# Seven products instead of eight in five chunks of two projections of a two-layer encoder

## The chip, the cores and the metric

The kernel runs on one core of a Trainium2 chip. The metric is the device time of one execution, in microseconds. Before the change it was measured three times: 2317.64, 2317.91 and 2318.44 us, median 2317.91. The five engines are called by the short names of the profile: PE (matrix multiply), DVE (VectorE), ACT (ScalarE), POOL (GpSimd) and SP (the engine that issues most transfers).

## What is computed

A trunk of two layers over x of 2048 tokens by 1024 features, in float32. Layer 0 mixes with a short gated convolution and a Fourier mixer, layer 1 with grouped-query attention:

```python
x = x + short_conv_fourier_mixer(rms_norm(x, norm_even), w_in_even, conv_w, w_out_even)
x = x + gqa_axial_mixer(rms_norm(x, norm_odd), w_in_odd, q_gain, k_gain, w_out_odd)
return rms_norm(x, final_norm)
```

The change concerns three of the four big matrix products in it: the output projection of layer 0 (`y @ w_out_even`, 2048x1024 by 1024x1024), the input projection of layer 1 (`h @ w_in_odd`, to q, k, v and the gate z, 2560 columns) and the output projection of layer 1 (1024 columns). The input projection of layer 0 already uses the scheme that the change brings to others.

## The kernel before, in words

**Chunks.** All big projections are cut into chunks of 1024 tokens (two blocks of 512, numbered `pr`) by 512 output columns. The contraction has 1024 features. So a chunk multiplies a 2x2 block matrix of activations (A11, A12, A21, A22: token block, then half of the features) by a 2x2 block matrix of weights (W11 to W22: half of the features, then half of the columns). `multiply` (L332) makes one block product: 4 slices of the contraction, 2 tiles of PSUM, and 3 matmuls each, since a float32 operand is kept as a rounded high word and a remainder (`split`, L40, a cast on ACT and a subtraction on DVE) and `mm3` (L56) adds high x high, high x low and low x high. That is 24 matmuls.

**Two ways to do a chunk.** `plain` (L368) makes the 8 block products of the schoolbook rule. `product` (L387) makes 7, by Strassen's rule in Winograd's form: beside A11, A12 and A22 it takes four combined activations, s3 = A11 - A21, s1 = A21 + A22, s2 = s1 - A11 = A22 - s3 and s4 = A12 - s2, and beside W11, W21 and W22 four combined weights t1 to t4 (`weight_ops`, L288, makes them with subtractions on POOL). The results of its products are summed on DVE (`sums`, L392) into tiles of the pool "e", before they are handed to the chunk's `out`, without PSUM for three of the four blocks. Before the change `product` is used in layer 0's input projection alone; the output projections and layer 1's input use `plain`.

**Rooms.** The pool "big" (tag "S") has 9 rooms of 16 KB a partition. An operand (high and low word) takes one. Two rooms are the rings "r" and "o": "r" has 4 places of 128x1024 for raw weights, "o" gives passing tiles by `pair` (L184), strictly in turn; in layer 0's input it has 3 places, the fourth holding a temporary of the combined weights, and after `renew` (L161) it has 4. The weights in use lie in the pool "w", 8 tiles (4 operands) in layers 0 and 1, 6 and two of another pool in the last projection. PSUM has 8 banks.

**What is done between products.** After each product `follow` (L361) calls a hook of the chunk and one step of `queue`. `queue_weights` (L310) puts the steps of the next chunk's weights there: the loads, and each of the four splits just after the product that uses the old block of that place for the last time. `reload` (L263) gives the hooks that load and split the next two token blocks. In layer 1, g1 scales the weights in the split (L285, L286).

**What sets the order.** The order of PE is that of the program text. The other engines and SP are ordered by a planner that simulates the program with its own times and prefers earlier text; every engine then runs its instructions strictly in that order. `issue_after` and `high_priority` bend this at a few places.

**The chunks in order.** Layer 0's output (`layer0_out`, L969) runs (pr, column half) = (0,0), (0,1), (1,0), (1,1). `out_chunk` (L933) loads the residual into a place of "o", adds it to PSUM on DVE (L945), stores x1, squares on ACT (L962) and adds up on POOL (L964). Layer 1's input (`layer1_in`) runs, for each pr, z2, kv, q0, q1, z3 (numbers 2, 4, 0, 1, 3); the very last, z3 of pr 1, is split into a batch and fillers that end inside the first steps of attention. In q and kv chunks the activations are the stationary side; `rope` works on DVE, ACT and POOL, and transposes on PE (`turn`, L1058) follow three or four products later. Layer 1's output (`layer1_out`) starts right at the end of attention and ends with a chunk cut by columns.

Of the kernel before, what the change touches and what calls it, by code (L numbers as in the profile page):

```python
# [23 lines left out]
P = 128  # L24
# [123 lines left out]
class Pairs:  # L148
# [7 lines left out]
    def __init__(self, c):  # L156
        self.c, self.nc = c, c.tc.nc
        self.A, self.pending, self.queue, self.rooms = {}, [], [], []
        self.renew(3)

    def renew(self, o=4):  # L161
        self.A.clear()
        self.size = {"r": 4, "o": o}
# [99 lines left out]
    def reload(self, src, name):  # L263

        return {i: lambda b=b: self.load_block(src, b, name) for i, b in ((0, "11"), (2, "12"), (4, "21"), (5, "22"))}
# [22 lines left out]
    def weight_ops(self, src, name, raw_tiles=None, lo_engs={}):  # L288
# [19 lines left out]
        return W, {"11": s11, "t2": s_t2, "t3": s_t3, "t1": s_t1, "21": s21, "t4": s_t4, "22": s22}  # L308

    def queue_weights(self, src, name, g):  # L310

        W, raw = {}, {}

        def start():
            raw.update(self.raw_weights(src))

        def step(b):
            return lambda: self.split_weights(W, b, raw[b], name, g=g)
# [4 lines left out]
        self.queue.extend([start, wait, step("11"), step("21"), wait, wait, step("12"), step("22")])  # L323
        return W

    def all_weights(self, src, name, lo_engs={}):
        W, steps = self.weight_ops(src, name, lo_engs=lo_engs)
# [59 lines left out]
    def product(self, W, out, name, hooks={}):  # L387
# [482 lines left out]
def layer0_out_start(c):  # L870
# [62 lines left out]
def out_chunk(c, pr, mc, W, hooks, conv_first, src, dst, acc, nm):  # L933
# [5 lines left out]
    def out(block, t, ps):  # L939
# [26 lines left out]
    st.plain(W, out, f"po{nm}_{pr}_{mc}_", hooks, conv_first)  # L966


def layer0_out(c):  # L969
# [801 lines left out]
```

## Time and profile before

| what | value |
|---|---|
| median of three runs | 2317.91 us |
| the profiled execution | 2315.25 us, its span 2313.5 us |
| layer 0's output projection | 583 to 760 us of the span |
| layer 1's input projection, up to attention | 760 to 1203 us |
| attention | 1203 to 2120 us |
| layer 1's output projection | 2120 us to the end |
| granted clock of PE, mean | 0.991 |
| bytes moved by DMA | 413.98 MB |

The profile shows one execution. Busy time is the union of an engine's instructions in a stretch; a wait is the idle time of an engine ahead of an instruction, put down to what ended it. Stretches are given in us from the start of the span. For a transfer, the time from its issue to its landing is given.

### The profile page before, as it was taken

The page shows a single profiled execution, that of the slowest core. Times are in us where ns is not written, and L with a number is a line of the kernel's source. Part 1 is how long each engine was busy: PE and PEld are TensorE (multiplying, and loading weights), DVE is VectorE, ACT ScalarE, POOL GpSimd, SP SyncE. Part 2 cuts the span into 40 slices and gives each one's busy share as a digit, 9 for nine tenths or more (in the row PEclk, how much of TensorE's full clock was granted, in tenths as well). Part 3 has the DMA queues.
Part 4 walks back from the last instruction along what each step waited for, and adds up shares of the span by engine and source line. Part 5 has one row for each costly group of instructions (what it writes and reads, how often), then busy time and mean ns, then how long its engine had stood idle before and what let it go on. Part 6 is the DMA issues. An engine that isn't in the chain of part 4 may idle for free. (4 is left out here: it accounts for less than half of the span.)

```text
span 2313.5 us, 34304 instructions
## 1 busy us (share of the span) xinstructions
PE 2265.7 (98%) x12450; PEld 1920.2 (83%) x12450; DVE 1530.3 (66%) x2479; ACT 1198.4 (52%) x2638; POOL 574.8 (25%) x408
## 2 busy tenths in 40 slices
PE   9999999998999999999999999999999999999998
PEld 7877778886888899889987888888888888888887
DVE  7967667679542545424537887788788778878235
ACT  5442333224332335424537777777777777777212
POOL 3566535444222222203211110000000110003212
PEclk9999999998999999999999999999999999999999
DMA  4244742265856533533465555555555555558653
GB/s 166 81 151 169 249 137 74 64 248 186 277 182 191 151 133 122 164 110 127 145 221 216 204 203 192 200 202 195 195 200 201 193 198 200 204 183 295 210 190 129
DMA packets 247992, 413.98 MB, mean 179 GB/s; under 512 B 24848, under 2 KB 144784, under 8 KB 246032
## 3 DMA queue, kind: packets, MB, share of 16 engines
q1 hardware_dynamic: 240944, 404.11, 51.0%
q0 software_dynamic: 1008, 6.55, 0.8%
q8 instruction: 99, 1.62, 0.3%
q10 hardware_dynamic: 5872, 1.14, 0.2%
q14 instruction: 69, 0.57, 0.1%
HBM read 190.92 MB, written 86.59 MB: 120 GB/s over the span
## 5 line engine op out<-in xcount | busy, mean ns | idle before, releaser
L1320 DVE TENSOR_REDUCE mx<-s 128x1 f32<-128x512 f32 x512 | 350.9, 686 | 173.7 <-PE s L60 173.3
L1339 ACT ACTIVATE praw<-s,nb,qs 128x512 f32<-128x512 f32 x512 | 400.6, 798 | 19.5 <-DVE nb L1329 13.4
L1362 ACT CAST pr<-t 128x512 fp32r<-128x512 f32 x512 | 290.0, 599 | 182.3 <-PE t L1350 182.3
L1366 DVE TENSOR_TENSOR pr<-t,pr 128x512 fp32r<-128x512 f32 x512 | 329.1, 679 | 7.5 <-ACT pr L1362 7.3
L1350 PEld LDWEIGHTS t<-ident_r,P 128*128 128x128 f32 x2048 | 202.0, 140 | 36.8 <-DVE pr L1366 1.1
L58 PE MATMUL s<-kv,aq 128*128 128x512 f32 x512 | 211.5, 413 | 3.1 <-DMA aq<-qT 1.9
L58 PE MATMUL o<-pr,kv 128*128 128x512 f32 x512 | 212.1, 414 | 0.1
L1350 PE MATMUL t<-ident_r,P 128*128 128x128 f32 x2048 | 203.8, 243 | 0.9 <-DVE pr L1366 0.9
L60 PE MATMUL o<-pr,kv 128*128 128x512 f32 x512 | 202.5, 395 | 0.0
L60 PE MATMUL s<-kv,aq 128*128 128x512 f32 x512 | 202.5, 395 | 0.0
L59 PE MATMUL o<-pr,kv 128*128 128x512 f32 x512 | 202.1, 395 | 0.0
L59 PE MATMUL s<-kv,aq 128*128 128x512 f32 x512 | 201.3, 393 | 0.0
L1411 POOL TENSOR_TENSOR az<-az,lb 128x512 f32<-128x512 f32 x32 | 61.8, 1930 | 442.6 <-DMA lb<-ld 407.3
L964 POOL TENSOR_TENSOR acc<-acc,sq 128x512 f32<-128x512 f32 x48 | 69.2, 1442 | 214.5 <-ACT sq L962 196.3
L60 PEld LDWEIGHTS o<-pr,kv 128*128 128x128 f32 x512 | 96.2, 188 | 23.3
L60 PEld LDWEIGHTS s<-kv,aq 128*128 128x128 f32 x512 | 96.4, 188 | 22.6
L58 PEld LDWEIGHTS s<-kv,aq 128*128 128x128 f32 x512 | 95.9, 187 | 22.1 <-ACT praw L1339 3.2
L1418 POOL TENSOR_TENSOR az<-az,oc 128x512 f32<-128x512 f32 x32 | 42.2, 1318 | 286.2 <-ACT oc L1417 286.1
L1339 ACT ACTIVATION_READ_ACCUMULATOR praw<-s,nb,qs 128x1 f32 x512 | 112.2, 219 | 0.0
L59 PEld LDWEIGHTS s<-kv,aq 128*128 128x128 f32 x512 | 96.6, 189 | 17.3
L59 PEld LDWEIGHTS o<-pr,kv 128*128 128x128 f32 x512 | 96.5, 188 | 17.2
L58 PEld LDWEIGHTS o<-pr,kv 128*128 128x128 f32 x512 | 96.0, 187 | 16.9 <-ACT oc L1417 0.2
(643 smaller groups left out, 5821.9 us busy)
## 6 DMA issues: line engine op xcount, KB each, us to landing
P<-praw SPq DMA_DIRECT2D x256, 512.0 KB, 3.2
ring_r<-w SPq DMA_DIRECT2D x80, 512.0 KB, 3.6
ring_o<-x_T SPq DMA_DIRECT2D x32, 512.0 KB, 4.8
ring_r<-wo SPq DMA_DIRECT2D x32, 512.0 KB, 7.0
qT<-ring_o SPq DMA_DIRECT2D x64, 256.0 KB, 2.8
aq<-qT SPq DMA_DIRECT2D x31, 512.0 KB, 4.6
x1T<-po_t SPq DMA_DIRECT2D x16, 512.0 KB, 3.9
a_x<-x1T SPq DMA_DIRECT2D x16, 512.0 KB, 4.4
```

What stands on the lines that cost most here:

```text
L58: nc.tensor.matmul(ps, lh, rh, start=first, stop=False, skip_group_check=shared)
L59: nc.tensor.matmul(ps, lh, rl, start=False, stop=False, skip_group_check=shared)
L60: nc.tensor.matmul(ps, ll, rh, start=False, stop=last, skip_group_check=shared)
L964: nc.gpsimd.tensor_tensor(a, a, sq, op=ALU.add)
L1320: self.nc.vector.tensor_reduce(st.mx[h][:, b:b + 1], st.banks[h, b][:], op=ALU.max, axis=AX.X)
L1339: self.exp = nc.scalar.activation(raw[:, b % 2], st.banks.pop((h, b))[:], AF.Exp, bias=st.nb[h][:], scale=self.c.qs[:, st.g[0], st.g[1], h ...
L1350: self.nc.tensor.transpose(pt[:, h * P:(h + 1) * P].bitcast(F32R), st.Ps[h // 2][:, h % 2, kt // 8, (kt % 8) * P:(kt % 8 + 1) * P], self.c ...
L1362: self.nc.scalar.copy(pr[:, 0], pt[:])
L1366: self.nc.vector.tensor_tensor(pr[:, 1], pt[:], pr[:, 0], op=ALU.subtract)
L1411: nc.gpsimd.tensor_tensor(zt, zt, rb[:].rearrange("p (t h) -> p h t", h=4), op=ALU.mult)
L1418: nc.gpsimd.tensor_tensor(st.zt[:], st.zt[:], o[:], op=ALU.mult)
```

## The change

Five chunks take `product` instead of `plain`: (0,1) and (1,1) of layer 0's output, z3 of pr 0 and z2 of pr 1 of layer 1's input, and (0,1) of layer 1's output. `prepare` is new: during the chunk in front (for the z chunks, the two q chunks in front) it makes s3, s2, s1 and s4 from the activations in DRAM. s3 overwrites a passing tile, from which s2 is made; half by half s2 is also stored in DRAM ("spill") and read back for s4, which takes the room of A21 once that was used for the last time. `queue_weights` now also makes combined weights, over the end of the chunk in front and the first three products of the fast one, and in layer 1 scales the raw blocks in place on ACT first. `product` with `last` lets go of each operand at its product; the reloads of the next token blocks hang on the first four products of the fast chunk. For pr 1, layer 1's order becomes kv, q0, q1, z2, z3. The ring "o" has 3 places throughout. Two stores bring the last slice of the Fourier result to yT in DRAM, where `prepare` reads it.

```diff
-    def renew(self, o=4):
+        self.renew()
+
+    def renew(self):
         self.A.clear()
-        self.size = {"r": 4, "o": o}
+        self.size = {"r": 4, "o": 3}
...
+    def prepare(self, src, name):
+
+
+        nc = self.nc
+        halves = [slice(0, 2), slice(2, 4)]
+        spill = self.c.dram.tile([2, P, 2, TB], F32, name=f"s2_{name}", tag=f"s2_{name}")
+
+        def room(op, b, k):
+
+            if op not in self.A:
+                self.A[op] = self.atile(f"a{op}_{name}")
+            self.fetch(self.raw(op, k), src, b, k)
+            return self.raw(op, k)
+
+        def s32(i):
+            k, t = halves[i], self.pair()
+            self.fetch(t, src, "21", k)
+            nc.gpsimd.tensor_tensor(t, room("s3", "11", k), t, op=ALU.subtract)
+            a22 = room("s2", "22", k)
+            self.put("s3", k, t)
+            nc.vector.tensor_tensor(t, a22, t, op=ALU.subtract)
+            self.put("s2", k, t)
+            nc.sync.dma_start(spill[i], t)
+
+        def s1():
+            for k in halves:
+                t = self.pair()
+                self.fetch(t, src, "22", k)
+                nc.gpsimd.tensor_tensor(t, room("s1", "21", k), t, op=ALU.add)
+                self.put("s1", k, t)
+
+        def s4():
+            self.A.pop("21")
+            for i, k in enumerate(halves):
+                t = self.pair()
+                nc.sync.dma_start(t, spill[i])
+                nc.gpsimd.tensor_tensor(t, room("s4", "12", k), t, op=ALU.subtract)
+                self.put("s4", k, t)
+
+        return lambda: s32(0), lambda: s32(1), s1, s4
...
-    def queue_weights(self, src, name, g):
-
-        W, raw = {}, {}
...
+    def queue_weights(self, src, name, g=None, now="plain", then="plain", rooms=()):
...
         def start():
-            raw.update(self.raw_weights(src))
-
-        def step(b):
-            return lambda: self.split_weights(W, b, raw[b], name, g=g)
+            if then == "plain":
+                raw.update(self.raw_weights(src))
+            else:
+                ops["W"], ops["steps"], ops["raw"] = self.weight_ops(src, name)
...
+        def scale(*blocks):
+            for b in blocks if g is not None else ():
+                for i in range(4):
+                    k = 4 * (int(b[0]) - 1) + i
+                    self.nc.scalar.activation(ops["raw"][b][:, i], ops["raw"][b][:, i], AF.Copy, scale=g[:, k:k + 1])
...
+        def step(op):
+            def run():
+                if op in rooms:
+                    self.rooms.append(tuple(self.lp.tile([P, 4, TB // 2], F32R, tag="w0", name=f"{name}_{op}{n}") for n in "hl"))
+                if then == "plain":
+                    self.split_weights(W, op, raw[op], name, g=g)
+                else:
+                    scale(*{"11": ["11"], "t2": ["12", "22"], "21": ["21"]}.get(op, ()))
+                    ops["steps"][op]()
+                    W.update(ops["W"])
+            return run
...
-        self.queue.extend([start, wait, step("11"), step("21"), wait, wait, step("12"), step("22")])
+        first = [step(op) for op in (("11", "21", "12", "22") if then == "plain" else ("11", "t2", "t3", "t1", "21", "t4", "22"))]
+        if now == "plain":
+            self.queue.extend([start, wait, first[0], first[1], wait, wait, first[2], first[3]] + first[4:])
+        else:
+            last = self.queue.pop()
+            self.queue.extend([lambda: (last(), start())] + first)
         return W
...
-    def product(self, W, out, name, hooks={}):
...
-        ps = {}
+        ps, A = {}, self.A
+        if last:
+            A = dict(self.A)
+            self.A.clear()
         for a in ("11", "s2", "s3", "s1", "12", "22", "s4"):
             base = ps.get({"12": "11", "s4": "s1"}.get(a))
-            ps[a] = self.multiply(self.A[a], W[W_OPS[a]], f"{name}{a}", base, a in ("11", "s1"))
+            ps[a] = self.multiply(A.pop(a) if last else A[a], W[W_OPS[a]], f"{name}{a}", base, a in ("11", "s1"))
...
     def step5():
         for j, op in enumerate(("12", "22")):
+            nc.sync.dma_start(c.yT[j, 7], c.y_last[:, j])
             after = st.put(op, 3, c.y_last[:, j])
...
         def add(o, x):
-            for i in range(2):
-                nc.vector.tensor_tensor(o[:, i], x[:, i], ps[i][:], op=ALU.add)
+            if ps:
+                for i in range(2):
+                    nc.vector.tensor_tensor(o[:, i], x[:, i], ps[i][:], op=ALU.add)
+            else:
+                nc.vector.tensor_tensor(o, t[:], x, op=ALU.add)
...
-    st.plain(W, out, f"po{nm}_{pr}_{mc}_", hooks, conv_first)
+    if kind == "plain":
+        st.plain(W, out, f"po{nm}_{pr}_{mc}_", hooks, conv_first)
+    else:
+        st.product(W, out, f"po{nm}_{pr}_{mc}_", hooks, True)
...
+    kinds = ("plain", "fast", "plain", "fast", "plain")
...
-        Wn = st.queue_weights(c.wo0[1 - mc], f"wo0_{i + 1}", None) if i < 3 else st.queue_weights(c.w1[2], "w1_0", c.g1)
-        hooks = {}
-        if i == 1:
-            hooks = st.reload([c.yT[2], c.yT[3]], "y1")
-        if i == 2:
-            hooks = {0: lambda: rstd(0), 2: lambda: rstd(1)}
-        if i == 3:
-            hooks = st.reload([c.x1T[0], c.x1T[1]], "x0")
-        out_chunk(c, pr, mc, W, hooks, i == 0, c.x_T, c.x1T, acc, "0")
+        src, name, g = (c.wo0[1 - mc], f"wo0_{i + 1}", None) if i < 3 else (c.w1[2], "w1_0", c.g1)
+        Wn = st.queue_weights(src, name, g, kinds[i], kinds[i + 1])
+        if mc == 0:
+            s3a, s3b, s1, s4 = st.prepare([c.yT[2 * pr], c.yT[2 * pr + 1]], f"y{pr}")
+            hooks = {0: s3a, 2: s3b, 4: s1, 6: s4}
+            if pr:
+                hooks.update({0: lambda: (rstd(0), s3a()), 1: lambda: rstd(1)})
+        else:
+            src, name = ([c.yT[2], c.yT[3]], "y1") if pr == 0 else ([c.x1T[0], c.x1T[1]], "x0")
+            hooks = st.reload(src, name, ("11", "s2", "s3", "s1"))
+        out_chunk(c, pr, mc, W, hooks, kinds[i], c.x_T, c.x1T, acc, "0", i == 0)
         W = Wn
...
+            if ps:
+                for i in range(2):
+                    nc.vector.tensor_tensor(t[:, i], ps[i][:], RB[tb], op=ALU.mult)
+            else:
+                nc.vector.tensor_tensor(t[:], t[:], RB[tb].unsqueeze(1).broadcast_to([P, 2, TB]), op=ALU.mult)
...
+        if kind == "plain":
+            st.plain(W, out, f"pz{zc}_{pr}_", hooks)
+        else:
+            st.product(W, out, f"pz{zc}_{pr}_", hooks, pr == 0)
+
+    chunks = [(n, 0) for n in (2, 4, 0, 1, 3)] + [(n, 1) for n in (4, 0, 1, 2, 3)]
     W = c.w1_first
+    kind = ["fast" if i in (4, 8) else "plain" for i in range(10)]
...
-        Wn = st.queue_weights(c.w1[chunks[i + 1][0]], f"w1_{i + 1}", c.g1)
+        Wn = st.queue_weights(c.w1[chunks[i + 1][0]], f"w1_{i + 1}", c.g1, kind[i], kind[i + 1])
         if n == 4:
             tables(pr, c.kg, f"k{pr}")
             kv_chunk(pr, W)
-        elif n < 2:
-            if n == 0:
-                tables(pr, c.qg, f"q{pr}")
-            q_chunk(pr, n, W)
+        elif n == 0:
+            tables(pr, c.qg, f"q{pr}")
+            s3a, s3b, s1, s4 = st.prepare([c.x1T[2 * pr], c.x1T[2 * pr + 1]], f"x{pr}")
+            q_chunk(pr, n, W, {1: s3a, 3: s3b, 6: s1})
+        elif n == 1:
+            q_chunk(pr, n, W, {6: s4})
         elif i == 0:
             z_chunk(pr, n - 2, W, {1: lambda: c.rstd1(2), 3: lambda: c.rstd1(3)})
         else:
-            z_chunk(pr, n - 2, W, st.reload([c.x1T[2], c.x1T[3]], "x1") if i == 4 else {})
+            src = [c.x1T[2], c.x1T[3]]
+            hooks = st.reload(src, "x1", ("11", "s2", "s3", "s1")) if i == 4 else {"s3": lambda: st.load_block(src, "21", "x1")}
+            z_chunk(pr, n - 2, W, hooks, "fast")
...
-    def room(i):
-        st.queue.insert(2, lambda: st.rooms.append(tuple(lp.tile([P, 4, TB // 2], F32R, tag="w0", name=f"wo1_{i}_{n}") for n in "hl")))
...
+    st.lp = lp
+    kinds = ("plain", "fast", "plain", "plain")
...
-        hooks = {}
-        Wn = st.queue_weights(c.wo1[1 - mc], f"wo1_{i + 1}", None)
-        room(i + 1)
+        Wn = st.queue_weights(c.wo1[1 - mc], f"wo1_{i + 1}", None, kinds[i], kinds[i + 1], ("11", "21") if i == 0 else ("21",))
+        if i == 0:
+            s3a, s3b, s1, s4 = st.prepare(src, "o0")
+            hooks = {0: s3a, 2: s3b, 4: s1, 6: s4}
         if i == 1:
-            hooks = {**st.reload([c.oT[2], c.oT[3]], "o1"), 7: lambda: load_x(2)}
+            hooks = {**st.reload([c.oT[2], c.oT[3]], "o1", ("11", "s2", "s3", "s1")), "22": lambda: load_x(2)}
         if i == 2:
             hooks = {0: lambda: (load_x(3), rstd(0)), 2: lambda: rstd(1), 4: lambda: finish(0)}
-        out_chunk(c, pr, mc, W, hooks, False, c.x1T if i < 2 else None, x2T if i < 2 else X2, acc, "1")
+        out_chunk(c, pr, mc, W, hooks, kinds[i], c.x1T if i < 2 else None, x2T if i < 2 else X2, acc, "1")
...
```

More of the change, by code (lines that the diff above doesn't have):

```diff
@@ L158, in __init__ @@
         self.A, self.pending, self.queue, self.rooms = {}, [], [], []
-        self.renew(3)
-    def renew(self, o=4):
+        self.renew()
+    def renew(self):
         self.A.clear()
-        self.size = {"r": 4, "o": o}
+        self.size = {"r": 4, "o": 3}
         self.rings, self.held, self.count = {}, set(), {"r": 0, "o": 0}
@@ L261, in load_block, with reload @@
             self.split(b, k)
-    def reload(self, src, name):
-        return {i: lambda b=b: self.load_block(src, b, name) for i, b in ((0, "11"), (2, "12"), (4, "21"), (5, "22"))}
+    def reload(self, src, name, keys=(0, 2, 4, 5)):
+        return {i: lambda b=b: self.load_block(src, b, name) for i, b in zip(keys, ("11", "12", "21", "22"))}
+    def prepare(self, src, name):
[30 more added lines that the diff above has]
+        return lambda: s32(0), lambda: s32(1), s1, s4
     def raw_weights(self, src, raw_tiles=None):
@@ L385, in plain, with product @@
             self.follow(hooks.get(i))
-    def product(self, W, out, name, hooks={}):
+    def product(self, W, out, name, hooks={}, last=False):
         c, nc = self.c, self.nc
@@ L930, in layer0_out_start, with out_chunk @@
     return {(2, 0): first, (2, 2): op11, (2, 3): split11, (3, 1): step1, (3, 2): step2, (3, 3): step3, 4: step4, 5: step5}
-def out_chunk(c, pr, mc, W, hooks, conv_first, src, dst, acc, nm):
+def out_chunk(c, pr, mc, W, hooks, kind, src, dst, acc, nm, conv_first=False):
     nc = c.tc.nc
@@ L1090, in kv_chunk, with q_chunk @@
         st.plain(W, out, f"pk{pr}_", hooks, rows=True)
-    def q_chunk(pr, qc, W):
+    def q_chunk(pr, qc, W, hooks):
         def out(block, t, ps):
@@ L1108, in out, with z_chunk @@
             turn(t, nm, (0, 1, 2, 3), save, 3)
-        st.plain(W, out, f"pq{qc}_{pr}_", rows=True)
-    def z_chunk(pr, zc, W, hooks={}):
+        st.plain(W, out, f"pq{qc}_{pr}_", hooks, rows=True)
+    def z_chunk(pr, zc, W, hooks={}, kind="plain"):
         def out(block, t, ps):
             tb, m = 2 * pr + int(block[0]) - 1, 4 * zc + 2 * (int(block[1]) - 1)
-            for i in range(2):
-                nc.vector.tensor_tensor(t[:, i], ps[i][:], RB[tb], op=ALU.mult)
+            if ps:
[3 more added lines that the diff above has]
+                nc.vector.tensor_tensor(t[:], t[:], RB[tb].unsqueeze(1).broadcast_to([P, 2, TB]), op=ALU.mult)
             nc.scalar.activation(t[:], t[:], AF.Silu)
@@ L1120, in z_chunk @@
         RB = {tb: bcast_d(c, c.RD[tb], f"n1_{zc}_{tb}") for tb in (2 * pr, 2 * pr + 1)}
-        st.plain(W, out, f"pz{zc}_{pr}_", hooks)
-    chunks = [(n, pr) for pr in range(2) for n in (2, 4, 0, 1, 3)]
+        if kind == "plain":
[3 more added lines that the diff above has]
+    chunks = [(n, 0) for n in (2, 4, 0, 1, 3)] + [(n, 1) for n in (4, 0, 1, 2, 3)]
     W = c.w1_first
+    kind = ["fast" if i in (4, 8) else "plain" for i in range(10)]
     for i, (n, pr) in enumerate(chunks[:-1]):
-        Wn = st.queue_weights(c.w1[chunks[i + 1][0]], f"w1_{i + 1}", c.g1)
+        Wn = st.queue_weights(c.w1[chunks[i + 1][0]], f"w1_{i + 1}", c.g1, kind[i], kind[i + 1])
         if n == 4:
```

6 lines of the change are left out of this document (3 added, 3 removed).

## The prediction

> **What bounds the kernel now.** I read the busy shares first, then the stretches of the chunks that the change touches, then the waits of TensorE (PE).
>
> ```profile
> PE 2265.7 (98%) x12450; PEld 1920.2 (83%) x12450; DVE 1530.3 (66%) x2479; ACT 1198.4 (52%) x2638; POOL 574.8 (25%) x408
> ```
>
> Busy time by stretch (length, then busy PE, PEld, DVE, ACT, POOL, then granted clock, DMA share, GB/s). The first eight are a chunk each, or two or three in a row, of the output and layer 1 projections; the last three are chunks of layer 0's input that already take 7 products.
>
> ```profile
> 583.07:627.11 44.04, 44.04 (x195) 36.14 (x194) 28.43 (x30) 19.39 (x24) 9.46 (x6) 1.00 0.86 301
> 627.11:671.06 43.95, 43.95 (x194) 36.06 (x192) 14.69 (x16) 12.88 (x17) 11.56 (x8) 1.00 0.62 201
> 671.06:759.85 88.79, 88.79 (x393) 72.90 (x392) 36.37 (x46) 28.99 (x43) 23.14 (x16) 1.00 0.58 187
> 850.34:945.33 94.99, 94.99 (x819) 94.99 (x818) 48.20 (x91) 48.94 (x181) 27.34 (x25) 1.00 0.40 131
> 945.33:991.04 45.71, 45.71 (x210) 37.72 (x209) 19.92 (x35) 15.87 (x36) 8.38 (x7) 1.00 0.58 184
> 1125.63:1172.72 47.09, 47.09 (x418) 47.09 (x417) 25.22 (x49) 25.91 (x96) 12.54 (x12) 1.00 0.54 176
> 2120.21:2164.95 44.74, 44.23 (x194) 35.98 (x192) 27.07 (x29) 20.92 (x27) 20.89 (x6) 1.00 0.80 279
> 2164.95:2208.89 43.94, 43.94 (x193) 36.06 (x192) 12.57 (x15) 10.92 (x15) 11.56 (x8) 1.00 0.61 201
> 357.66:396.11 38.45, 38.45 (x169) 31.55 (x168) 26.42 (x30) 11.30 (x14) 16.84 (x9) 1.00 0.21 68
> 434.56:473.02 38.46, 38.46 (x170) 31.55 (x168) 25.70 (x28) 11.32 (x14) 16.58 (x9) 1.00 0.19 61
> 231.30:279.00 47.70, 42.49 (x170) 33.59 (x169) 29.55 (x28) 20.17 (x24) 24.36 (x17) 0.93 0.91 302
> ```
>
> In every touched chunk PE is busy for the whole stretch at full clock, while DVE has half of it free or more. The order of PE is written by hand, so a matmul less is its pitch less, as long as nothing else becomes late.
>
> **What is removed.** A plain chunk has 8 products of 24 matmuls, a fast one 7. Two products apart:
>
> ```profile
> 605.14 0.39 PE L58 MATMUL po<-a_y,wo_12h 128*128 128x512 f32 x1
> 616.13 0.39 PE L58 MATMUL po<-a_y,wo_12h 128*128 128x512 f32 x1
> ```
>
> 10.99 us for 48 matmuls is 0.229 us each, 5.49 us a product. A fast chunk of 7 is then 38.45 us, which the rows at 357.66 and 434.56 show to the hundredth. Five chunks lose 5 x 5.49 = 27.5 us.
>
> **What is added, and where it lies.** Durations:
>
> ```profile
> L44 DVE TENSOR_TENSOR a_y<-a_y 128x1024 fp32r<-128x1024 f32 x7 | 8.5, 1220 | 2.4 <-ACT a_y L42 2.4
> L42 ACT CAST a_y<-a_y 128x1024 fp32r<-128x1024 f32 x6 | 6.3, 1051 | 6.8 <-DMA a_y<-yT 6.8
> L300 POOL TENSOR_TENSOR ring_r<-ring_o,ring_r 128x1024 f32<-128x1024 f32 x5 | 13.0, 2608 | 0.1
> L395 DVE TENSOR_TENSOR pa_u<-pa_p,pa_s 128x512 f32<-128x512 f32 x8 | 5.4, 684 | 3.0 <-PE pa_s L60 2.8
> L44 DVE TENSOR_TENSOR w_21l<-ring_r,w_21h 128x1024 fp32r<-128x1024 f32 x5 | 12.6, 2519 | 0.0
> a_y<-yT SPq DMA_DIRECT2D x6, 512.0 KB, 9.1
> ```
>
> For one fast chunk: s2, s3, s1 and s4 take 8 splits (8 x 1.22 = 9.8 us DVE, 8.4 us ACT), 2 subtractions on DVE (2.4) and 6 on POOL (6 x 2.61 = 15.6). Its weights take 7 splits for 4 (3.7 DVE, 3.2 ACT) and 4 subtractions on POOL (10.4); in layer 1 the gain is applied in place on ACT first, and 7 wide DVE splits stand for 16 narrow ones, about even. The sums take 10 DVE additions from PSUM (6.8) and 2 ACT copies, and three later additions lose their PSUM operands (1.22 for 2 x 0.68, about -0.4 together). That is 22 us of DVE, 13 of ACT, 26 of POOL, and 16 transfers of 512 KB (12 loads, 2 stores of the spilled half and 2 loads of it), 8.4 MB, each with an issue on SP. The two new stores of y_last (256 KB each) are alone of their kind.
>
> All of it has the chunk in front and the fast chunk itself for cover, some 82 us of PE. The fullest pair is the first: DVE 28.4 + 14.7 + 22.3 = 65 us of 82.5, POOL 9.5 + 11.6 + 26 = 47, ACT 45. Layer 0's fast chunks ran DVE 26.4 and POOL 16.8 in 38.45 without PE losing anything, so I take 0 for the engines' work. If that cover went, the excess over the stretch would be the price (below).
>
> The new waits: POOL's subtraction waits for two loads; behind it on POOL stand acc's additions and, in the q chunks, rope's small operations, for which the transposes on PE wait. The spill's store waits on SP for the chain load, POOL, ACT, DVE, DVE; behind it on SP stand residual loads and the next raw weights. s2 is wanted one product into the fast chunk, 632.6 in the first pair; from its loads' landing it takes 2.6 + 1.05 + 1.22 + 1.22 + 1.05 + 1.22 = 8.4 us, so the loads must land by 624. s1 has 11 us more, s4 27 us more.
>
> DMA in and before the first and the last pair:
>
> ```profile
> 582.00:598.00 16.00, 16.00 (x72) 13.17 (x71) 13.86 (x15) 8.41 (x10) 3.77 (x2) 1.00 1.04 373
> 598.00:620.00 22.00, 22.00 (x97) 18.04 (x97) 13.93 (x15) 9.90 (x13) 5.69 (x4) 1.00 0.88 301
> 620.00:627.00 7.00, 7.00 (x32) 5.75 (x31) 1.60 (x2) 1.05 (x1) 0.00 (x0) 1.00 0.35 125
> 2109.00:2131.00 22.00, 21.49 (x113) 17.57 (x112) 20.02 (x27) 18.23 (x29) 8.34 (x1) 1.00 1.06 383
> 2131.00:2164.00 33.00, 33.00 (x146) 27.07 (x145) 15.79 (x16) 11.39 (x14) 12.55 (x6) 1.00 0.72 246
> ```
>
> The first pair's front chunk moves 13.2 MB already. Of these the six a_y loads (3.1 MB) fetch the blocks of the pair after next ahead of time, into rooms that s3, s2 and s1 now take; so 10.1 MB + 6.3 MB for s3, s2 and s1, at 380 GB/s 43 us of 44. That can be late by little or nothing. Bounds for these two pairs: below, 0 (rows 357 to 473); above, the row at 231.30, a fast chunk at a DMA share of 0.91 throughout, 47.70 - 38.45 = 9.2 us over. The saturated part ends at 620 and 2131, so they are nearer to the lower end: 1 us each, 2 in all. The three other pairs start at shares of 0.58 or less: 0.
>
> **The edge to attention.** In the second half the z chunk moves behind the q chunks, so q's and k's stores end some 40 us earlier against the first scores.
>
> ```profile
> PE s L58 <- DMA aq<-qT: 1.9, 1, 1.9
> aq<-qT ACTq DMA_DIRECT2D x1, 512.0 KB, 5.8
> L1303 ACTq DMA_DIRECT2D aq<-qT x1: 359/359/359, 1197.4 to 1197.4; - x1
> 1200.00:1205.00 5.00, 3.07 (x14) 2.18 (x13) 0.67 (x1) 0.00 (x0) 0.00 (x0) 0.97 0.99 324
> 1205.00:1210.00 5.00, 5.00 (x17) 4.02 (x16) 3.15 (x7) 0.42 (x1) 0.00 (x0) 0.69 1.03 415
> ```
>
> PE waits 1.9 us for the first q load, and the clock falls to a mean of 0.69 in the 5 us after, another 1.5. The load is issued late (1197.4) and lands among kv loads, in 5.8 us against the 3.6 that a load of this size takes on a quiet queue (row under (b)); with kv's words stored earlier those loads can go ahead of it, which is worth 2.2 us there. Against that, the fast z chunk keeps 7 operands in the rooms that kv needs; s3's and s1's come free after 16.5 and 22 us of its 38.45, with half a chunk (22 us) still to come. Bounds -3.4 (the wait goes, with its clock) and +3.4 (a second such wait); I take half of the gain, -1.7.
>
> **The sum** is made against the profiled execution, 2315.25 us (span 2313.5): 2315.25 - 27.5 + 2 - 1.7 = 2288.1. The median of the runs stands 2.66 above that execution: 2290.7, say 2291.
>
> **Rivals.**
>
> (a) DVE and POOL get in each other's way. The w_21l row is the same split as a_y's, beside a POOL subtraction: 2.52 us for 1.22. If all 26 us of new POOL work pushed DVE back, the pairs would need, against their stretch less a product: first 43.1 + 22.3 + 26 = 91.4 of 82.5; second 36.4 + 48.3 = 84.7 of 83.3; last 39.6 + 48.3 = 87.9 of 83.2; the q pairs, with three chunks for it (68 + 48 of 135), nothing. Late by 9 + 1 + 5 = 15 us: 2306. Against it: 26.42 + 16.84 = 43.3 us in 38.45 (357.66) with PE whole. The Trainium skill (SBUF — State Buffer, "Who interferes with whom") says that a DVE instruction with two SBUF inputs and a GpSimd instruction that reads SBUF exclude each other, the first holding the pair for its whole length; the w_21l row agrees. By that rule alone this rival would be the forecast, but the row at 357.66 shows that only part of the work meets.
>
> (b) The ring "o" has 3 places for 4, and a spilled pair holds one for load 3.6, the 8.4 above and store 3.6, 15.6 us. Rope's last POOL operation and its transposes:
>
> ```profile
> 889.10 1.38 POOL L1048 TENSOR_TENSOR pq_t<-pq_t,ring_o 128x512 f32<-128x512 f32 x1
> 902.65 1.04 PE L1058 MATMUL ptq<-ident,pq_t 128*128 128x128 f32 x8
> ring_r<-w SPq DMA_DIRECT2D x80, 512.0 KB, 3.6
> ```
>
> The margin is 902.65 - 890.48 = 12.2 us, so a rope behind a spill can cost 3.4 us; two in each q chunk that has spills, four in all: 14 us, 2305. Residual additions have PSUM for most of a chunk behind them, more margin.
>
> (c) Slower: SP stands at the spills. At a landing of 9.1 us a spill keeps SP for 9.1 + 8.4 = 17.5 us; over the same margin of 12.2 PE loses 5.3, and with the clock's fall as at 1205 (1.5) 6.8 us a spill. There are ten; with more than five of them SP has eaten the gain, with all ten the time is 2291 + 68 = 2359, with seven 2339. For it: the planner sets SP's order from its own times, and these stretches run at 9.1. Against it: SP already holds waits of this kind (stores of x1T behind DVE, every chunk) and PE loses nothing to them in the rows above.
>
> (d) The transfers come late at both saturated places, by the full 9.2 each, and the edge adds 3.4 in place of -1.7: 2291 + 16.4 + 5.1 = 2312.
>
> **Chances.** Forecast (2285 to 2297) 0.70; (a) or (b) or part of them, to 2307, 0.15; (d) 0.05, half of it within 0.2%; (c) 0.05; better than 2285 (other waits at the edges go too) 0.05. A measurement tells 0.2% (4.6 us) from no change; so faster 0.92, same 0.03, slower 0.05. The range of 8 in 10 takes in the forecast and most of (a) and (b): 2284 to 2305.
>
> **What would show it.** PE's matmuls 5 x 24 = 120 fewer (12450 to about 12330), the fast chunks 38.5 us long at po, pz with t and s operands, no row of PE waiting on a DVE or ACT split between the first output chunk and attention; DVE 20 us a pair more. (a) would show w_t or a_s splits of 2 us and more, with PE waiting for them; (b) PE waiting at ptq; (c) SP waiting at the spill with ring_o or ring_r loads next. I am wrong if the sum of PE's waits in the five pairs is over 10 us.

## The result, and the profile after

The changed kernel takes 2345.23 us (2344.47 to 2351.38 in four runs) where the kernel before took 2318.01 on the same chip: a ratio of 1.0123, 95% interval 1.0106 to 1.0141. It is 1.2% slower; 2291 was forecast, and the range ended at 2305. Its profiled execution took 2344.58 us, 29.3 more than that of before. What was to go did go. The page of the changed kernel, busy time and instructions of each engine:

```profile
PE 2251.1 (96%) x12330; PEld 1905.7 (81%) x12330; DVE 1694.0 (72%) x2557; ACT 1264.6 (54%) x2713; POOL 720.9 (31%) x458
```

The 120 matmuls are gone. But PE had been idle 2313.5 - 2265.7 = 47.8 us of its span before and is idle 91.7 us now, and DVE and POOL have 164 and 146 us more to do. PE's busy time fell by 14.6 us, not by the forecast 27.5: behind its waits it ran at a lower granted clock, as the rows below show. Where that idle time lies is read from the stretches of the changed kernel (length; busy PE, PEld, DVE, ACT, POOL; granted clock, DMA share, GB/s). In order: output (0,0), (0,1), (1,0), (1,1), the first z chunk, z3 of the first half, and layer 1's output (1,0).

```profile
584.38:635.08 50.70, 46.61 (x196) 37.42 (x195) 37.20 (x30) 19.51 (x24) 30.58 (x13) 0.93 0.78 279
635.08:673.53 38.45, 38.45 (x170) 31.57 (x168) 33.94 (x32) 20.81 (x25) 16.89 (x8) 1.00 0.91 317
673.53:728.52 54.99, 46.54 (x201) 37.93 (x200) 31.67 (x26) 16.33 (x21) 37.03 (x19) 0.94 0.85 232
728.52:768.72 40.20, 39.00 (x170) 31.41 (x169) 28.76 (x30) 19.75 (x26) 14.03 (x7) 1.00 0.84 288
768.72:822.05 53.33, 46.39 (x202) 37.89 (x200) 28.17 (x43) 16.29 (x33) 18.14 (x14) 0.94 0.71 210
965.24:1010.84 45.60, 42.32 (x187) 34.37 (x186) 36.84 (x40) 23.09 (x41) 19.59 (x10) 0.96 0.82 263
2224.15:2283.40 59.25, 47.80 (x201) 38.91 (x200) 31.62 (x36) 12.82 (x20) 18.06 (x13) 0.88 0.80 247
```

The first fast chunk runs in 38.45 us to the hundredth. The three longest stretches, 54.99, 53.33 and 59.25 us for some 44.8, are not fast chunks at all. They are the plain chunks **behind** one. Together they lose 33.0 us. PE's waits in the changed kernel (in all, times, longest):

```profile
PE pm_n L96 <- POOL acc L1037: 26.8, 3, 11.4
PE ptq L1137 <- POOL pq_t L1127: 6.2, 3, 3.1
PE po L59 <- DVE a_y L44: 4.1, 1, 4.1
PE pz_s L58 <- DVE pz_u L461: 2.6, 1, 2.6
```

In the kernel before, PE waited neither for POOL's sums in acc nor at ptq. pm_n are the four transposes of `rstd_d`, by which the squares that POOL adds up in acc become the row factors of the next norm. Their place on PE is written in the text. Those of a pair's first token block, the only ones that PE waits for, stand after the first product of the chunk behind a fast one in both output projections, and after the second in the first z chunk. The timeline of the changed kernel around the first of them, PE's instructions and then POOL's:

```profile
678.79 0.40 PE L60 MATMUL po<-a_y,wo_11l 128*128 128x512 f32 x1
687.63 1.11 PE L96 MATMUL pm_n<-ident,acc 128*128 128x128 f32 x4 [8.45 <-POOL acc L1037]
...
670.51 10.33 POOL L1037 TENSOR_TENSOR acc<-acc,sq 128x512 f32<-128x512 f32 x5
680.81 3.32 POOL L285 TENSOR_TENSOR ring_o<-as_y,ring_o 128x1024 f32<-128x1024 f32 x1
684.09 3.49 POOL L1037 TENSOR_TENSOR acc<-acc,sq 128x512 f32<-128x512 f32 x2
```

A plain chunk hands out its blocks spread over its length. A fast one does not: three of its four blocks come out after its 5th, 6th and 7th product, and the first after its 4th. So six of a fast chunk's eight additions to acc fall due in its last two products or behind them. The order of the blocks matters as much. In `plain`, the last block of the first token block comes out after the 6th of 8 products; in `product` that block (12) is the very last. In the kernel before, POOL had finished the first token block's sum at 666.2, 10.3 us before its transposes:

```profile
664.93 1.30 POOL L964 TENSOR_TENSOR acc<-acc,sq 128x512 f32<-128x512 f32 x1 [0.31 <-ACT sq L962]
```

In the changed kernel PE wants this sum at 679.2, 5.6 us into the chunk, and starts on it at 687.6; POOL has the subtraction of the next preparation in the middle of its additions. At the two other places no subtraction stands on POOL. There the last sums come late on DVE, behind splits for the chunk that is running. In the first z chunk (768.72) PE allows two products, 11.1 us, and still waits 6.9, since DVE comes to the last block's sums 10.4 us after the last product:

```profile
770.49 4.80 DVE L328 SCALAR_TENSOR_TENSOR w_21l<-ring_r,g1s,w_21h 128x256 fp32r<-128x256 f32 x4
...
779.13 1.27 DVE L461 TENSOR_TENSOR po_u<-po_u,po_s 128x512 f32<-128x512 f32 x2
```

The additions themselves are stretched. The groups of that line, minimum, median and maximum of one in ns, first in the kernel before:

```profile
L964 POOL TENSOR_TENSOR acc<-acc,sq x48: 1285/1301/2172, 605.3 to 2269.6; 128x512 f32<-128x512 f32 x48
```

and in the changed kernel, with the split of the combined operands on DVE:

```profile
L1037 POOL TENSOR_TENSOR acc<-acc,sq x48: 1260/1482/2332, 612.8 to 2293.6; 128x512 f32<-128x512 f32 x48
L44 DVE TENSOR_TENSOR as_y<-ring_o,as_y x16: 1210/1226/3426, 597.8 to 742.9; 128x1024 fp32r<-128x1024 f32 x16
```

Beside POOL operations the split takes up to 3.43 us instead of 1.22. POOL's addition has a median of 1.48 us instead of 1.30; its longest is 2.33, where it was 2.17 before.

### The profile page after: what moved, and what is told of

Read it like the earlier page. It is cut to its first block, busy times and chain, and to the rows that moved or that the text cites. A ratio compares the mean times of both kernels' runs of the same rounds, so it can differ in the third digit from the quotient of the medians.

```text
span 2342.8 us, 34481 instructions
## 1 busy us (share of the span) xinstructions
PE 2251.1 (96%) x12330; PEld 1905.7 (81%) x12330; DVE 1694.0 (72%) x2557; ACT 1264.6 (54%) x2713; POOL 720.9 (31%) x458
## 5 line engine op out<-in xcount | busy, mean ns | idle before, releaser
L1508 POOL TENSOR_TENSOR az<-az,oc 128x512 f32<-128x512 f32 x32 | 41.3, 1291 | 288.6 <-ACT oc L1507 288.6
L1037 POOL TENSOR_TENSOR acc<-acc,sq 128x512 f32<-128x512 f32 x48 | 81.5, 1700 | 129.4 <-ACT sq L1035 113.8
```

Source lines behind the costliest of these rows:

```text
L1037: nc.gpsimd.tensor_tensor(a, a, sq, op=ALU.add)
L1508: nc.gpsimd.tensor_tensor(st.zt[:], st.zt[:], o[:], op=ALU.mult)
```

## The experiments

All but two start from the changed kernel; each was compared with the kernel before on the same chip (2317.3 to 2319.3 us). The chunk lengths below are differences of the starts of their first products.

### Two suspects: the place of the transposes, and POOL beside DVE

e1 moves the transposes (and with them the finish that follows them) later:

```diff
-hooks.update({0: lambda: (rstd(0), s3a()), 1: lambda: rstd(1)})
+hooks.update({3: lambda: rstd(0), 5: lambda: rstd(1)})
...
-{1: lambda: c.rstd1(2), 3: lambda: c.rstd1(3)}
+{4: lambda: c.rstd1(2), 6: lambda: c.rstd1(3)}
...
-{0: lambda: (load_x(3), rstd(0)), 2: lambda: rstd(1), 4: lambda: finish(0)}
+{0: lambda: load_x(3), 3: lambda: rstd(0), 5: lambda: rstd(1), 7: lambda: finish(0)}
```

e2 leaves them and makes the combined activations on DVE instead of POOL; e3 does both; e4 also makes the weights' combinations of the five chunks on DVE.

```diff
-nc.gpsimd.tensor_tensor(t, room("s3", "11", k), t, op=ALU.subtract)
+nc.vector.tensor_tensor(t, room("s3", "11", k), t, op=ALU.subtract)
...
-self.nc.gpsimd.tensor_tensor(out, a, b, op=ALU.subtract)
+(self.nc.vector if diff_dve else self.nc.gpsimd).tensor_tensor(out, a, b, op=ALU.subtract)
```

> The changed kernel with the transposes of the sums of squares later in their chunk: in (1,0) of layer 0's output and of layer 1's output after the fourth and the sixth product (they stood after the first and the second or third), in the first z chunk after the fifth and the seventh (second and fourth); finish of the first token block after the eighth. Theory P (the place is the cause: the fast chunk hands its blocks out over its last four products, and the eight additions to acc end only 14 to 17 us into the next chunk): the three waits of 26.8 us go with the half clock behind them, 33 us in chunk lengths; 2345 - 33 = 2312, same or slightly faster than before. Theory Q (POOL and DVE are too full in the chunk behind, since preparation shares them): POOL stays behind and the waits move with the transposes; less than half of the 33 us comes back, 2330 or more.

> The changed kernel with the six combining operations of each preparation on DVE instead of POOL; the transposes stay where the change has them. Theory Q: POOL loses 15 us a pair, acc's additions are no longer behind 2.5 to 3.3 us subtractions, and DVE's splits no longer stretch beside them: the waits at the transposes fall by more than half, those at ptq and in the first chunk go; 2320 to 2325. Theory P: the last block's additions still end after the first product of the next chunk (sums, residual, squares and two additions, 9.5 us after the products against 5.5), so the waits shrink to 4 us each but the clock still falls; 2330 to 2336.

> Both: transposes later, and preparation's six operations on DVE. If P and Q each own a part, this has neither the 33 us of the transposes nor the waits at ptq (6.2 us) and at the a_y split in the first chunk (4.1 us, 6.7 in the chunk's length): 2345 - 33 - 15 = 2297. If Q was nothing, it equals e1 (2312) or is slower by what DVE loses.

> As e3, and the four subtractions of the combined weights of the five new fast chunks on DVE too, so that POOL has no more work than in the kernel before. If two-input work on DVE and POOL's reads hold each other up, DVE's splits fall back to 1.22 us and the waits in z3 of pr 0 (5.4 us in the chunk's length) go: 2290 to 2295. If DVE is simply full by then (some 34 us added a pair), new waits of PE at sums and splits: 2300 or more.

Measured: e1 2347.58 us (1.0115, 1.0098 to 1.0133), e2 2339.7 (1.0082, 1.0065 to 1.0100), e3 2325.56 (1.0029, 1.0018 to 1.0039), e4 2317.95 (0.9991, 0.9980 to 1.0002). Each misses the gain that its theory hoped for, e4 by over 20 us. In e2 the waits for pm_n stay whole (27.4 us in all), where both of its theories had them shrink; the waits at ptq for POOL go. Neither cause alone carries the loss. In e1 the waits for pm_n are gone, the three chunks take 44.9 us each, and nothing is won. Its waits:

```profile
PE po L60 <- DVE wo_22l L44: 11.6, 1, 11.6
PE ptq L1137 <- POOL pq_t L1127: 6.1, 3, 3.2
PE po L58 <- ACT wo_21h L42: 5.2, 1, 5.2
```

The stall went on to the next thing that was short of time: the weights of the fast chunk behind (55.8 us instead of 38.5) and the last weights of all.

All of the combining on DVE was then tried without the late transposes:

> The changed kernel with all of its new combining (operands and weights) on DVE and the transposes where the change has them. If the two causes act each by itself, the 13.1 us that DVE gave over the late transposes alone (6 us for the operands, 7.6 us for the weights) come off 2345: 2332 us. If POOL is late only because of the combining (then the place of the transposes is no cause of its own): 2320 us or less, and the waits for pm_n are under 3 us each. If the place sets it alone: 2340 us or more, waits for pm_n of 8 us or more.

e16 takes 2327.26 us (1.0038, 1.0024 to 1.0051), 18.0 less than the changed kernel. That is more than the 13.1 expected. The waits at ptq and for a_y and pz_u shrink to 0.3 us and less. The additions to acc are as slow as in the changed kernel (median 1.48 us, longest 3.82), and the place stays a cause of its own:

```profile
PE pm_n L96 <- POOL acc L1037: 23.6, 3, 8.1
```

Its timeline, in the order of the work from the last sum of the fast chunk, whose last matmul starts at 670.16, to the transposes:

```profile
675.52 0.68 DVE L461 TENSOR_TENSOR po_u<-po_u,po_s 128x512 f32<-128x512 f32 x1
676.12 1.71 DVE L44 TENSOR_TENSOR wo_22l<-ring_r,wo_22h 128x1024 fp32r<-128x1024 f32 x1
677.75 1.21 DVE L1018 TENSOR_TENSOR po_u<-po_u,ring_o 128x1024 f32<-128x1024 f32 x1
...
679.06 1.15 ACT L1035 ACTIVATE sq<-po_u 128x512 f32<-128x512 f32 x2 [2.37 <-DVE po_u L1018]
...
679.76 3.66 POOL L1037 TENSOR_TENSOR acc<-acc,sq 128x512 f32<-128x512 f32 x2 [3.02 <-ACT sq L1035]
...
683.48 0.90 PE L96 MATMUL pm_n<-ident,acc 128*128 128x128 f32 x3 [7.44 <-POOL acc L1037]
```

From the last product to the complete sum it takes 13 us, and PE allows 5.6. The steps themselves (two sums, the residual, a square, two additions of 1.30 us undisturbed) are 2 x 0.68 + 1.21 + 0.6 + 2.60 = 5.8 us: here nothing is left for what stands between them on DVE.

### A milder move of the transposes

e5 changes the order of the two token blocks in it: the one whose sums are complete first is transposed after the second product, the other after the fourth; the finish follows that order. e6 and e7 add the steps of e2 and e4, and e8 also calls the first preparation's hooks after the second, fourth, fifth and seventh product instead of the first, third, fifth and seventh. The edit at the first of the three places:

```diff
-hooks.update({0: lambda: (rstd(0), s3a()), 1: lambda: rstd(1)})
+hooks.update({1: lambda: rstd(1), 3: lambda: rstd(0)})
```

> The changed kernel with the two token blocks' transposes in the other order, since the fast chunk hands out block 12 last: the second token block's after the second product, the first's after the fourth, at all three places; in layer 1's output finish of the second block takes the old place (after the fifth product) and ring o, finish of the first moves into the column part and takes ring r. Theory P: the waits of 26.8 us go, and since the DRAM round trip of the result is no later than 5.5 us against the kernel before, no other wait comes in their place (in e1_late it did: finish after the eighth product held SP and DVE, and wo_22 and wo_t1 came late); 2345 - 33 = 2312. Theory Q: POOL's backlog moves the wait to wo_t1 of the fast chunk of (1,1) again; 2325 or more.

> e5_swap with preparation's six operations on DVE. P and Q each own a part: the ptq waits (6.2 us and the clock behind them) go as in e2_dve; 2300 to 2303. If the port is the matter and not POOL's queue, the same.

> e6_swap_dve with the four subtractions of the new combined weights on DVE: POOL has the work of before. From e4_late_dve_all's trace (2318, span 2310.7): its chunks beyond their products lose 2.3 us in the first chunk, 7.8 behind wo_t1, 1.8 in z3 and 12.3 behind finish; the second and the last of these should go: 2295 to 2299.

> e7 with the first preparation one product later in the text (after the second, fourth, fifth and seventh product), so that the planner puts DVE's splits of the first chunk's own operands ahead of it: the wait at the a_y split (1.7 us in e4) goes with the clock behind it, 2 us less than e7. If the wait comes from transfers and not from the order on DVE, equal to e7.

Measured: 2342.09 (1.0105, 1.0089 to 1.0122), 2329.46 (1.0049, 1.0034 to 1.0064), 2323.84 (1.0028, 1.0018 to 1.0039) and 2328.18 us (1.0035, 1.0024 to 1.0047). The waits for pm_n fall to 3 to 5 us in all; as in e1 others take their place (in e7 wo_12l 6.5, wo_t1 7.1). The hooks of e8 gain nothing. e5 came out as its theory Q had it, above 2325; e6 and e7 missed theirs by some 25 us. The milder move is no better than the late one: the intervals of e5 and e1 overlap, so do those of e6 and e3, and e7 is 6 us slower than e4.

### Where the stall had gone

e4 has two large holes left: 14 us in the last part and 7.9 us in (1,1). The first is read from its timeline (DVE, PE):

```profile
2234.45 4.07 DVE L1564 SCALAR_TENSOR_TENSOR ring_o<-ring_o,gfs,rb_n 128x512 f32<-128x512 f32 x6 [16.06 <-DMA rb_n<-rd_n]
...
2257.55 2.74 DVE L1564 SCALAR_TENSOR_TENSOR ring_r<-ring_r,gfs,rb_n 128x512 f32<-128x512 f32 x4 [10.95 <-DMA rb_n<-rd_n]
...
2262.73 1.69 DVE L44 TENSOR_TENSOR wo_22l<-ring_r,wo_22h 128x1024 fp32r<-128x1024 f32 x1
...
2264.47 0.80 PE L60 MATMUL po<-a_o,wo_22l 128*128 128x512 f32 x1 [11.54 <-DVE wo_22l L44]
```

DVE stands twice at the first operation of a `finish`, which waits for the row factors to go through DRAM and back: 16.06 us for the first token block and 10.95 us for the second. The split of the last weights is behind both in DVE's order, and the second wait ends 5.2 us before it. e10 sends both behind that split; e9 does this and also sends the broadcast loads of the first z chunk behind the stores of (1,1).

```diff
-            hooks = {0: lambda: load_x(3), 3: lambda: rstd(0), 5: lambda: rstd(1), 7: lambda: finish(0)}
+            hooks = {0: lambda: load_x(3), 3: lambda: rstd(0), 5: lambda: rstd(1)}
...
-        if m == 1:
-            finish(1)
+        if m < 2:
+            with c.tc.issue_after(st.last_w[1]):
+                finish(m)
```

> As the 2317.95 us kernel, only the finish of the first two token blocks sent behind the split of the last weights. Theory: PE's wait for wo_22l in the column part goes (11.5 us) and the waits for wo_t1 in the fast output chunk stay: 2317.95 - 12 = 2306 us, ratio 0.995. Rival (volume of work, not order): another weight or operand is late by as much, 2315 to 2318 us.

> All of the combining on DVE and the transposes late, as in the 2317.95 us kernel, and two orders changed: the finish of the first two token blocks is sent behind the split of the last weights, and the broadcast loads of the first gate chunk are sent behind the last store of the chunk in front. Theory (what is left of the loss is a queue that stands while the 512 small words of the row factors make their round trip through memory: rd_n lands 10 to 13 us after its issue, and rb_n at the head of SP and then of DVE waits for it): PE's wait for wo_22l (11.5 us) and the two for wo_t1 (2.9 and 2.6 us, with the half clock 7.8 us) go; 2317.95 - 12 - 7 = 2299 us, ratio 0.992, faster than both kernels. Rival (the weights are late because ACT and DVE have too much to do there, whatever the order): PE waits for another weight or operand in their place, no more than 5 us are gained, 2313 us.

e10 takes 2302.83 us (0.9930, 0.9904 to 0.9955), 15.1 less than e4: the first four columns fall from 36.2 us to 22.0, and the wait is gone. e9 takes 2302.09 (0.9929, 0.9907 to 0.9951): the order of the broadcast loads changed nothing that shows, (1,1) still takes 45.9 us. That half of my theory fell. ACT's timeline in e9 shows what is late there:

```profile
730.42 1.04 ACT L42 CAST as_y<-ring_o 128x1024 fp32r<-128x1024 f32 x1 [19.09 <-DVE ring_o L304]
731.37 1.04 ACT L42 CAST wo_t1h<-ring_r 128x1024 fp32r<-128x1024 f32 x1
```

ACT stands 19.09 us at the split of s4, the operand that PE wants last, and t1's, wanted fourth, is behind it. s4 needs the spilled s2 (s_y) and A12 (as_y). The DMA issues of e9 between 700 and 732 us (count, KB, median us to landing):

```profile
ring_o<-s_y SPq DMA_DIRECT2D x2, 512.0 KB, 14.1
as_y<-yT SPq DMA_DIRECT2D x2, 512.0 KB, 17.1
```

The second half of s_y, issued at 710.8, and the first of A12, issued at 712.1 and the last that this split waits for, both landed after 16.7 to 16.8 us. In the same stretch lie the two stores of row factors (`rd_n`, 512 words of 4 bytes each), issued at 703.5 and 711.7. e12 issues those on POOL's queue instead of SP's; e13 does that alone to the changed kernel, e14 alone to the kernel before.

```diff
-    nc.sync.dma_start(d[0:nj].rearrange("j t -> t j"), r[:, 0:nj])
+    nc.gpsimd.dma_start(d[0:nj].rearrange("j t -> t j"), r[:, 0:nj])
```

> As the 2302.09 us kernel (late transposes, combining on DVE, the two orders), only the small store of the row factors (rd_n, 512 words) issued by POOL on its own queue instead of SP. Theory (on SP's queue the transfers issued behind rd_n land with or after it: s_y issued 0.5 us behind it landed after 11.3 us, the next after 16.8 us, and ACT stands 19 us at the split of that operand, with wo_t1's behind it): the s_y loads land within 6 us, PE's waits for wo_t1 go, the second fast chunk takes 38.5 to 39.5 instead of 46.0 us, 2302 - 7 = 2295 us, ratio 0.990. Rival (the DMA engines are full there, or the small words slow every queue alike): s_y still lands after 10 us or more and the time stays at 2300 to 2303 us.

> The changed kernel, only the small store of the row factors on POOL's queue. Theory (there the transposes that stand too early and POOL's work beside DVE set the time, and the store comes after them): 2345 - 2 = 2343 us, within 2340 to 2346, PE's three waits for pm_n stay. Rival (the store is the main loss from the start): below 2330 us.

> The kernel before, only the small store of the row factors on POOL's queue. Theory (its PE waits for nothing there): 2318 us, within 0.1%. Rival (the store costs the kernel before as much as the changed one, so that its removal is no part of what the change needs): 2310 us or less.

e12 takes 2301.71 us (0.9934, 0.9919 to 0.9948): no gain, the rival held. The same view of e12:

```profile
ring_o<-s_y SPq DMA_DIRECT2D x2, 512.0 KB, 11.0
as_y<-yT SPq DMA_DIRECT2D x2, 512.0 KB, 18.3
rd_n<-rs POOLq DMA_DIRECT2D x2, 2.0 KB, 13.6
```

The queue is not the cause: loads on SP's queue land as late beside small stores on POOL's (the first s_y, issued before either store, took 5.5 us, the second 16.6). e13 takes 2344.28 us (1.0120, 1.0103 to 1.0137) and e14 2319.04 (1.0008, 0.9998 to 1.0017), both as my theory had them: the store's queue is no part of the loss. So e15 leaves the store on SP and takes one of the two out of the stretch. The transposes and the factors stay; the second block's store is issued behind the last operand load of (1,1), at 744.6, some 30 us later.

```diff
+    def store1():
+        with c.tc.issue_after(st.last_fetch):
+            nc.sync.dma_start(c.RD[1][0:4].rearrange("j t -> t j"), c.rs[1][:, 0:4])
...
+            if pr:
+                hooks["12"] = store1
```

> As the 2302.09 us kernel, only the store of the second token block's row factors (rd_n, 512 words; the transposes and the factors themselves stay) is issued behind the last operand load of the second fast output chunk, some 40 us later. Theory (whatever is in flight beside a store of 512 words lands with it, 11 to 19 us after its issue, on any queue): with one store instead of two in the stretch s4's loads land before 718 us into the span, PE's waits for wo_t1 go, that chunk takes 38.5 to 39.5 instead of 46.0 us: 2302 - 7 = 2295 us, ratio 0.990. Rival (the loads are late there for another reason): s_y and as_y land as late as before, 2300 to 2303 us.

e15 takes 2296.75 us, 0.9907 (0.9888 to 0.9926) of the kernel before. This interval overlaps that of e9, so the times alone do not show the gain; the chunk does. The same view of e15:

```profile
ring_o<-s_y SPq DMA_DIRECT2D x2, 512.0 KB, 7.9
as_y<-yT SPq DMA_DIRECT2D x2, 512.0 KB, 9.8
```

Its trace tells the landing of the second s_y alone: 7.9 us, where it was 16.8. (1,1) of e15 takes 38.46 us with no wait:

```profile
716.39:754.85 38.46, 38.46 (x170) 31.55 (x168) 31.69 (x33) 21.01 (x29) 8.39 (x5) 1.00 0.97 282
```

This DMA share of 0.97 is the highest of any fast chunk shown, and PE loses nothing. The loads still took 7.9 us and more, and s4's last ones landed at 720.6 to 724.3, not before 718 as I had put it. That moving one store out from beside the loads takes the wait away is shown by this pair of traces; why a store of 2 KB does that to loads on another queue isn't.

### The ring

e11 is the kernel before with three places in the ring "o", nothing else.

```diff
-    def renew(self, o=4):
+    def renew(self, o=3):
```

> The kernel before, with three places instead of four in the ring o of the output and layer 1 projections, and nothing else. Rival (b) of the prediction (a write into the ring waits for the transposes two products later, 3.5 us each at four q chunks): 2318 + 14 = 2332 us, ratio 1.006, with waits of PE for pq_t. Theory (the ring has little part in the loss, the waits for pq_t come from POOL being stretched and fuller): under 3 us, 2318 to 2321 us.

2319.72 us, 1.0005 (0.9993 to 1.0016). PE has no wait for ptq at all.

### The ledger

| us | forecast | changed | e16 | e4 | e15 |
|---|---|---|---|---|---|
| output (0,0) | 44.0 | 50.7 | 45.0 | 46.3 | 45.9 |
| output (0,1), fast | 38.5 | 38.5 | 38.5 | 38.5 | 38.5 |
| output (1,0), transposes | 44.8 | 55.0 | 54.1 | 44.9 | 44.8 |
| output (1,1), fast | 38.5 | 40.2 | 40.7 | 46.3 | 38.5 |
| z2 first half, transposes | 44.9 | 53.3 | 55.4 | 44.8 | 44.9 |
| kv, q0, q1 first half | 140.6 | 143.2 | 140.6 | 140.6 | 140.6 |
| z3 first half, fast | 40.2 | 45.6 | 41.0 | 42.0 | 41.3 |
| kv, q0, q1, z2 second half | 176.2 | 185.1 | 181.8 | 178.4 | 181.8 |
| layer 1's output (0,0), (0,1) | 83.2 | 83.4 | 83.2 | 83.2 | 83.2 |
| layer 1's output (1,0), transposes | 44.8 | 59.3 | 54.9 | 44.9 | 44.8 |
| its first four columns | 24.1 | 22.0 | 22.0 | 36.2 | 22.0 |

The forecast column is the trace before with 5.5 us taken from each fast chunk. Read across: from 2345 us, combining on DVE takes 18 (e16), the late transposes 9 more (e4; 30 gained in three places, 20 lost again in two), the finish behind the weights 15 (e10), the second store out of the way some 5 (e15 against e9, with overlapping intervals). Over the rows the changed kernel is 56 us above the forecast.

## Why the prediction was wrong

**Right: what is removed.** 120 matmuls and 5.49 us a chunk; the fast chunks of the output projections run at 38.45 to 38.46 us wherever nothing is late. (The five chunks lie in three projections, not two as the title has it.) With the four repairs 21.8 of the 27.5 us arrive (2296.75 for 2318.54). In that kernel's profile the output projection began 4.1 us later than in that of before; such starts lie between 583.1 and 588.2 us in the kept profiles.

**The step that failed** is "so I take 0 for the engines' work", reached by setting the engines' busy time against 82 us of PE as cover. In place of the 0 the runs show two prices: 18 us for the combining on POOL (e16), and, with the combining on DVE, 30 us in three chunks for the place of the transposes (e16 against e4). The sum of busy times does not say when PE asks. The prediction named acc's additions ("behind it on POOL stand acc's additions") and gave them no price, because it did not follow who reads acc, and when. Two facts of the kernel were wanted: that a fast chunk hands out its blocks late, the one that is wanted first at the very end (its code says after which product), and that the transposes stand 5.6 us into the next chunk, 11.1 in the first z chunk (the hooks say so). The chain from the last product to the sum is 5.8 us by its own durations (e16's rows above), so in the output projections it was late even if nothing came between. With what stood between on DVE, and at the first place on POOL too, it was late by 7 to 11 us, three times.

**Rival (a)**, DVE and POOL in each other's way, was priced at 15 us; taking the combining off POOL gave 18 (e16). That the totals are so close is in part luck: the places differ. (a) had 9, 1 and 5 us in the first, second and last pair and nothing in the q pairs; e16 gives back 5.7, 0.5 and 0.2 there, some 10 in the q pairs and 4.4 in layer 1's output (1,0), and the first z chunk gets 2 us slower. Nor does e16 tell the two engines' hold on each other from POOL's queue, since it takes both away. The sign came at another split than those I had named, in the first chunk, where PE waited 4.1 us for a_y:

```profile
597.84 3.43 DVE L44 TENSOR_TENSOR as_y<-ring_o,as_y 128x1024 fp32r<-128x1024 f32 x1
601.19 2.82 DVE L44 TENSOR_TENSOR a_y<-ring_r,a_y 128x512 fp32r<-128x512 f32 x1
```

POOL had subtractions of 2.87 and 3.31 us from 597.3 to 603.5. In e16, with none beside them, the same two splits took 1.22 and 0.68. I had taken 0.15 for (a) and (b) together; (a) was no alternative to the forecast's other losses but came on top. The Trainium skill (SBUF — State Buffer, "Who interferes with whom") has a DVE instruction with two SBUF inputs contend with a GpSimd instruction that reads SBUF, over a port pair that is locked exclusively. The trace agrees in kind: the two splits ended 1.1 and 0.6 us after the POOL subtractions beside them. But half of the 16 splits took 1.23 us or less, so the median is no guide to the places where it hurts.

**Rival (b)** is out: three places cost the kernel before 0.05%, within the uncertainty (e11), and e16, with three places and the spills in them, has no wait at ptq for POOL. The waits that I had given as its sign came from rope's POOL work, slowed and late: they go as soon as the preparation's six operations leave POOL (e2). A sign that two rivals share tells nothing.

**Rival (c)**, SP standing at the spills, did not happen as told: no wait of PE in the changed kernel is put down to a transfer behind a spill. Its price for seven spills, 2339 us, and for ten, 2359, bracket the measured time by luck alone. (By its own figures, 6.8 us a spill, four spills eat the gain of 27 us, not more than five.) In the repaired kernels the spill's read-back and the load beside it were late, beside the stores of row factors. **(d)**: the first pair's front chunk lost 6.7 us, but 5.7 of them go when the combining leaves POOL (e16), so they were not the transfers'; the last pair lost 0.2. My 2 us for both stand near what is left.

**The edge to attention.** PE waits 1.5 instead of 1.9 us for the first q load, where I had put a gain of 1.7 with the clock. But it waits 2.5 to 2.9 us there in e4, e15 and e16, which have the same order, so no gain is shown.

**The bound I set** ("wrong if the sum of PE's waits in the five pairs is over 10 us") was the right one. The first four rows of waits above sum to 39.7 us; two of the three waits for pm_n (6.9 and 11.4) lie in the chunks behind the pairs, and without them 21.3 are left.

## What to carry to other kernels

When a change makes a step's results come out later and in a heap, follow each result to its reader and compare times there, in particular where the reader is on the bounding engine with its place fixed by the text, and look which of the results is wanted first; busy shares say nothing of it. A stall that is removed is worth only what the next thing short of time allows: moving the transposes gained 30 us in three places and gave 20 back in two, and only after the orders behind them were mended did the removed work show. A small store of scattered words cost the loads beside it time here (e9 and e12 against e15), so it is worth trying to keep such stores out of stretches in which loads are due.

## What the runs showed of the hardware

A store of 512 words of 4 bytes landed 10.0 to 16.6 us after its issue (e9, six of them). Four 512 KB loads issued within some 3 us of the second store of (1,0) took 16.7 to 17.5 us to land in e9 and 16.6 to 19.0 in e12, with the store on POOL's queue. Not every transfer beside such a store is so late: one issued 2.4 us ahead of that store in e9 took 9.7 us, and in the kernel before three of 512 KB, issued up to 2 us ahead of the store at 694.85, took 6.6 to 8.8 us.

A wait of 8.45 us in the changed kernel was followed by 2.8 us at a granted clock of 0.50, from 687.63 on. The chunk around it took 54.99 us instead of 44.84, so the wait cost 1.7 us more than its length:

```profile
688.40:690.40 2.00, 2.00 (x7) 1.61 (x6) 1.75 (x4) 1.05 (x1) 0.64 (x1) 0.50 1.06 399
```

And kv, q0 and q1 of the second half took 141.5 us in e15 and 138.1 in e4, both at full clock and without a wait of PE. That is most of what e15 still lacks in that row of the ledger. Its cause stays open, but it need not be the change: in the kernel before, the same three chunks took 140.6 us in the first half and 137.7 in the second.
